# Load order and weight preparation in the scan stage of a two-layer SSD and pooling step

## The chip, the cores and the metric

The program runs on one core of one Trainium2 chip. The metric is the device time of one execution in microseconds (us); a smaller time is better. The time before is the median of three runs. A core has TensorE (PE) for matrix products, VectorE (DVE), ScalarE (ACT) and GpSimd (POOL) for elementwise work, and SyncE (SP), whose instruction queue here does nothing but issue transfers (DMAs). Each engine works through its own queue in order; an instruction that waits holds up all behind it.

## The reference

One inference step of a two-layer trunk on 1024 prompt tokens and 64 new sample tokens (8 sequences of 8), model width 1024. Layer 0 is a Mamba-2 SSD mixer, layer 1 a multi-scale causal pooling mixer. Each is modulated by adaLN and added to a residual. Cut to what matters:

```python
for i in range(DEPTH):                                   # 2 layers
    mod = silu(c) @ ada_w[i] + ada_b[i]                  # adaLN: shift, scale, gate
    hn = rmsnorm(x, norm_g[i]) * (1 + scale) + shift
    out = ssd_branch(hn, ...) if i == 0 else pool_branch(hn, ...)
    x = x + (1 + gate) * out

# ssd_branch
z, xbc, dt = split(hn @ w_in)
conv = conv_b + sum(xp[:, k:k+L] * conv_w[k] for k in range(4)); new_conv = xp[:, -3:]
xs, B, C = split(silu(conv))
y, new_ssm = ssd_scan(xs, softplus(dt + dt_bias), -exp(a_log), B, C, state)   # 8 groups of 4 heads
gated = grouped_rmsnorm((y + d * xs) * silu(z)) * norm_g
out = gated @ w_out
# ssd_scan, per chunk of 128 tokens
y = (C B^T * decay) (x dt) + C exp(acum) h ;  h = exp(acum_end) h + B^T decay_end (x dt)
```

Returned are the outputs for prompt and sample tokens, the SSM states, the last three convolution inputs and the last fifteen pooling inputs of each sequence.

## The kernel before

All data are float32. The big products run as three products of a high part in the type float32r and the rest (`hi*hi`, `hi*lo`, `lo*hi`), so each weight block has to be split by ACT (the high half, a rounded copy) and DVE (the low half, the difference). Activations lie with features on the 128 partitions and the 1088 tokens in the free dimension; many products are made with a Strassen-like scheme on halves of 544 tokens.

The program has these stages: a front (norm, first adaLN blocks, gate and part of the input projection, to about 339 us of the span), the scan stage (339 to about 870 us), the rest of the SSD output projection (to about 1000 us), then the pooling layer.

**The scan stage** (`ssd_layer`, `scan`) loops over the 8 groups `g`, and in each over four phases `p` of 256 tokens. A phase does, in the program's order: `prep_step((g, p))`; fill units (`units(fill, a)`, then `b`, then `c`, the counts come from `PACE`); `scan_front(p+1)`, the transposes of the next phase; `scan_state(p)`, the state update; `scan_decay(p+1)`, the decay matrices of the next phase on ACT and DVE; `scan_y(p)`, the products that give the output; one adaLN block where `ADA` names the phase. At `p == 3` `silu_burst` and the front of the next group follow. A fill unit is one third of a 128-column tile of the input projection of the next group: 24 matmuls (`mm`), some 4 us of PE. Units are what keep PE busy while the scan's chain runs on ACT and DVE. From group 7 on, the units are products of the SSD output projection (`op`).

**Loads.** Nearly every transfer is issued from SP. The pieces named below are:
- `scan_ac` (L542): `acb`, the decay exponents of four heads and 256 tokens, broadcast to all 128 partitions. There is one `acb` buffer, so the next one waits for the last read of the one before, which is `cd` (L583) in `scan_decay`.
- `stream_raw` (L137, L141): the stream of weights through three `wr` buffers. Projection blocks (`wr<-win`) and adaLN blocks (`wr<-adaA`, `wr<-adaG`, two per adaLN block) share it in a fixed order. `stream_next` loads up to three items ahead when a projection tile starts; `ada_block` asks for its own two blocks when it comes to them (`stream_next_raw`).
- `xbd`: projection tiles that the front had made and stored (`MOVED`: tile 1 of groups 1 to 7 and tile 2 of group 7). `proj_group` loads them back (L430) when it passes their place.
- `ncT` (L407): the convolution's edge rows, stored when the last tile of a group is done; they are copied by POOL (L371, L372).
- `hpT` (L606): the final prompt state of a group, stored in `scan_state` at `p == 3`.
- `prep_step`: prepares the first 8 of 28 weight blocks of the output projection, in 16 halves. A half is loaded as two blocks of 256 KB (`wp<-wout`, L1195); DVE adds or subtracts them (L1186) at the next call; at the call after that ACT makes the high half (L1181), DVE the low half (L1182), and 512 KB are stored (`wpd<-wp`, L1183). `PREP` says how many halves start at which call. `ow_load` loads the results back from group 7 on.

**What sets the order.** In the scan stage the PE queue is pinned to the program's order. The other queues are ordered by the framework's scheduler: it plays the program through with a model of the hardware, and each queue takes, of the instructions that the model holds to be ready, the one that is first in the program. So an instruction's place in the program is a priority, and where the hardware is later than the model, the queue waits.

Of the kernel before, what the change touches and what calls it, by code (L numbers as in the profile page):

```python
# [38 lines left out]
PACE = (((0, 1, 1), (0, 1, 1), (0, 1, 1), (0, 1, 2)),) * 6 + (((0, 2, 2), (0, 2, 2), (0, 1, 2), (0, 1, 2)), ((0, 1, 1), (0, 1, 2), (0, 1, 0), (0, 1, 1)))  # L39
ADA = tuple((g, p) for g in range(7) for p in ((0, 1, 2) if g == 0 else (0, 2, 3) if g == 1 else (0, 2, 3) if g == 5 else (0,) if g == 6 else (0, 2)))  # L40
NPREP = 8
PREP = {None: 4, (0, 0): 2, (0, 1): 2, (0, 2): 1, (0, 3): 1, (1, 3): 1, (2, 3): 2, (3, 3): 2, (4, 3): 1}
OWTAGS = (("wr", "wr"), ("wh", "wl"), ("wh", "wl"))
NSLOT_A = 30
NSLOT_B = 7
# [66 lines left out]
class Build:  # L112
# [147 lines left out]
    def ada_block(self, src, raws=None):  # L260

        nc = self.nc
        own = raws = raws or (self.ada_load(src) if src is not None else None)
        raws = [t[:, :1024] for t in raws] if raws else [self.stream_next_raw().rearrange("p a m -> p (a m)") for _ in range(2)]
        pm = self.pp.tile([P, 512], F32, tag=self.amtag, bufs={"mm": 3, "y": 2, "tr": 2}[self.amtag], name=self.name("am"))
        for hh in range(2):
            for j in range(4):
                self.te.matmul(pm[32 * j:32 * j + 32, :256], self.scp[:, j + 4 * hh, :], raws[hh][:, 256 * j:256 * j + 256],
                                 start=(hh == 0), stop=(hh == 1), tile_position=(0, 32 * j))
        if own:  # L270
            self.slots.free(*own)
        mp = self.cp.tile([P, 256], F32, tag="mp", bufs=1, name=self.name("mp"))
        nc.scalar.activation(mp, pm[:, :256], AF.Copy)
        yield
        p2 = pm[:, 256:]
        for i in range(2):
            self.te.matmul(p2[:, 16 * i:16 * i + 9], mp[:, 128 * i:128 * i + 128], self.kc[:, K_SEL9:K_SEL9 + 9], start=True, stop=True)
        yield p2
# [98 lines left out]
    def proj_open(self, g):  # L377
# [2 lines left out]
        ncv = self.gp.tile([P, 4, 9, 3], F32, tag="ncv", bufs=2, name=self.name("ncv"))  # L380
        return dict(g=g, scv=scv, ncv=ncv, ti=(16 + g, 24 + g, 2 * g, 2 * g + 1), out=[])

    def proj_begin(self, G, ii):
        nc = self.nc
        raw = self.raw_tile()
        nc.gpsimd.memset(raw[:, 0:3], 0.0)
        nc.gpsimd.tensor_copy(raw[:, 1027:1115].rearrange("p (b w) -> p b w", w=11)[:, :, 0:3], G["scv"][:, ii])
        return raw

    def proj_end(self, G, ii, raw, ahead=False):  # L390
        dst = self.slots.get("xbc")
        self.conv_tile(G["ti"][ii], raw, dst, G["ncv"][:, ii])
        g, nt = G["g"], self.io["ncT"][G["g"]]
        if ahead:
            self.nc.scalar.activation(dst, dst, AF.Silu)
            self.nc.sync.dma_start(nt[:, ii], G["ncv"][:, ii])
            if (g, ii) in MOVED:
                self.nc.sync.dma_start(self.xbd[g, ii], dst)
                self.slots.free(dst)
                return  # L400
        G["out"].append(dst)
        if ii == 3 and not ahead:
            kept = [i for i in range(4) if (g, i) not in MOVED]
            for a in kept:
                if a - 1 not in kept:
                    n = next(i for i in range(a, 5) if i not in kept)
                    self.nc.sync.dma_start(nt[:, a:n], G["ncv"][:, a:n])  # L407

    def silu_burst(self, s):

# [13 lines left out]
    def proj_group(self, G):  # L424

        nc = self.nc
        for ii in range(4):
            if (G["g"], ii) in MOVED:
                dst = self.slots.get("xbc")
                nc.sync.dma_start(dst, self.xbd[G["g"], ii])  # L430
                G["out"].append(dst)
                continue
            w = self.stream_next()
            raw = self.proj_begin(G, ii)
            if (G["g"], ii) == (7, 3):

                ps = [self.mm_tile() for _ in CH]
                for k in range(8):
                    for c in range(3):
                        self.mm1(ps[c], w, k, self.hn[k], CH[c], k == 0, k == 7)  # L440
                    self.slots.free(*self.hn[k])
                    yield
                for c in range(3):
                    self.proj_evict(G, ii, raw, ps[c], c)
                yield
                return
            for c, (a, n) in enumerate(CH):
                ps = self.mm_tile()
                self.mm3(ps, w, self.hn, CH[c])
                self.proj_evict(G, ii, raw, ps, c)  # L450
                yield
# [136 lines left out]
    def scan_state(self, s, p):  # L588

        nc, gp = self.nc, self.gs  # L590
        _, xd, Bt, cd, _ = s.M[p]
        S = self.pp.tile([P, 512], F32, tag="S", bufs=1, name=self.name("S"))
        for cc in range(2):
            self.te.matmul(S[:, 256 * cc:256 * cc + 256], Bt[:, cc], xd[:, cc, 1].rearrange("p r q -> p (r q)"), start=True, stop=True)
        for cc in range(2):
            h, Sv = s.h[-1], S[:, 256 * cc:256 * cc + 256].rearrange("p (r q) -> p r q", r=4)
            hn = gp.tile([P, 4, 64], F32, tag="h", bufs=3, name=self.name("h"))
            if h is None:
                nc.vector.tensor_copy(hn, Sv)
            else:  # L600
                hd = gp.tile([P, 4, 64], F32, tag="hd", bufs=1, name=self.name("hd"))
                nc.gpsimd.tensor_tensor(out=hd, in0=h, in1=cd[:, :, cc].unsqueeze(2).to_broadcast([P, 4, 64]), op=ALU.mult)  # L602
                nc.vector.tensor_tensor(out=hn, in0=hd, in1=Sv, op=ALU.add)  # L603
            s.h.append(hn)
        if p == 3:
            nc.sync.dma_start(self.io["hpT"][s.g], hn.rearrange("p r q -> p (r q)"))  # L606

    def scan_evac(self, s, q, src, tok):
        y = s.xs[q]
# [566 lines left out]
    def prep_step(self, key):  # L1176
# [10 lines left out]
        new = []  # L1187
        for _ in range(min(PREP.get(key, 0), 2 * NPREP - self.prepn)):
            i, h = divmod(self.prepn, 2)
# [367 lines left out]
    def fills(self):  # L1557

        for g in range(1, 7):
            yield from self.proj_fill(g)  # L1560
        pr = self.proj_fill(7)
        yield from itertools.islice(pr, 9 - 3 * len([i for i in MOVED if i[0] == 7]))
        self.op_begin(0)
        self.optags = ("mm",)
        self.rows = [None] * 16
        blk = self.row_blocks(2, 3)
        for j, _ in enumerate(pr):
            if j == 4:
                self.ow_load()
            for _ in range(99 if j == 7 else 1):  # L1570
                next(blk, None)
            if j < 8:
                yield
        self.ow_load()
        self.x = [None] * 8
        yield from self.out_fill()

# [39 lines left out]
    def scan(self, s, fill):  # L1617

        g = s.g
        last, after = self.scans[g - 1] if g else None, self.scans[g + 1] if g < 7 else None  # L1620
        for p in range(4):
            a, b, c = PACE[g][p]
# [8 lines left out]
            self.scan_state(s, p)  # L1631
            if p < 3:
                self.scan_decay(s, p + 1)
                if p < 2:
                    self.scan_ac(s, p + 2)
                elif after:
                    self.scan_ac(after, 0)
            self.units(fill, b)
            if p == 3 and after:
                self.silu_burst(after)  # L1640
            self.scan_y(s, p, self.sample_y if p == 3 else None)
            if p == 2:
                self.sample_front(s)
                self.sample_inter(s)
# [7 lines left out]
            elif p == 3:  # L1652
                if g < 7:
                    self.sample_decay(s)
                else:
                    self.gate_rows(s)
            self.units(fill, min(c, 1))
            for _ in ada:
                pass
            if p == int(g == 7):  # L1660
# [14 lines left out]
            else:  # L1675
                r = c - min(c, 1)
# [328 lines left out]
```

## Time and profile before

| what | value |
|---|---|
| median of 3 runs | 1622.03 us (1621.26 to 1628.29) |
| the profiled execution | 1621.86 us, of which the span from the first to the last instruction is 1620.0 us |
| PE, DVE, ACT, POOL busy | 1568.6, 1307.7, 803.4, 491.8 us |
| moved by DMA | 295.80 MB, mean 183 GB/s |

How to read it: busy time is the time in which at least one instruction of the engine was under way. PE is the engine with the most. A wait belongs to the engine that waited and names what ended it. The page cuts the span into 40 slices of 40.5 us, so the scan stage is slices 9 to 22.

### The profile page before, as it was taken

How to read it: one execution, taken by the hardware profiler on the slowest of the kernel's cores; microseconds unless marked ns; L12 is line 12 of the kernel's file. 1: busy time of each engine (PE TensorE's matmuls, PEld its weight loads, DVE VectorE, ACT ScalarE, POOL GpSimd, SP SyncE). 2: the span in 40 equal slices, each digit the busy share in tenths (PEclk: the TensorE clock that was granted, in tenths of full speed). 3: DMA queues.
4: the chain of work that ended last, by engine and by line, in shares of the span. 5: the costliest groups of instructions: out<-in, count | busy, mean ns of one | idle time of the engine just before them, and what ended most of it. 6: DMA issues, size and time to landing. Idle time of an engine off the chain costs nothing.

```text
span 1620.0 us, 31607 instructions
## 1 busy us (share of the span) xinstructions
PE 1568.6 (97%) x12495; PEld 1508.3 (93%) x12495; DVE 1307.7 (81%) x2095; ACT 803.4 (50%) x1426; POOL 491.8 (30%) x508
## 2 busy tenths in 40 slices
PE   8999999997999999999998999999999999999997
PEld 6899999996988888988887999999999999999997
DVE  6876787857888889888896999888889867667876
ACT  6663343446667667666653367523232334233355
POOL 0134555511121221111110003765666640000231
PEclk9999999998999999999998999999999999999999
DMA  8422222378675675677889763233323379466673
GB/s 350 164 100 94 87 84 85 111 245 289 225 251 186 207 255 187 215 262 246 320 282 306 194 161 118 71 115 113 115 102 105 108 236 380 135 179 178 162 164 115
DMA packets 118651, 295.80 MB, mean 183 GB/s; under 512 B 22860, under 2 KB 46824, under 8 KB 118504
## 3 DMA queue, kind: packets, MB, share of 16 engines
q1 hardware_dynamic: 110440, 270.32, 48.8%
q0 software_dynamic: 5760, 19.01, 6.7%
q10 hardware_dynamic: 2304, 4.46, 0.7%
q8 instruction: 98, 1.61, 0.4%
q14 instruction: 49, 0.40, 0.1%
HBM read 222.93 MB, written 68.59 MB: 180 GB/s over the span
## 4 chain that ended last, share of the span: by engine, by line
PE 77%; DVE 7%; DMA 7%; ACT 5%; issue 2%; POOL 1%; SPq 0%; DVEq 0%; ACTq 0%; POOLq 0%
PE st L103 32%; PE mm L103 18%; PE op L103 15%; PE y L103 3%; DMA wp<-wout 2%; PE pl L103 2%; DMA acb<-acd 2%; PE S L103 2%; PE am L103 1%; ACT M L580 1%; DMA wr<-pout 1%; PE tr L103 1%; PE ms L103 1%; DVE raw L366 1%; PE tr L106 1%
## 5 line engine op out<-in xcount | busy, mean ns | idle before, releaser
L103 PE MATMUL op<-b,w 128*128 128x272 f32 x2688 | 350.0, 292 | 15.6 <-ACT w L1231 7.1
L103 PEld LDWEIGHTS op<-b,w 128*128 128x128 f32 x2688 | 343.4, 191 | 21.3 <-ACT w L1231 7.7
L103 PE MATMUL st<-hh,w 128*128 128x272 f32 x1664 | 323.2, 289 | 0.0
L103 PEld LDWEIGHTS st<-hh,w 128*128 128x128 f32 x1664 | 265.4, 189 | 0.3 <-issue 0.3
L103 PE MATMUL st<-t,w 128*128 128x272 f32 x1872 | 242.7, 288 | 1.3 <-POOL w L197 1.3
L103 PE MATMUL st<-hl,w 128*128 128x272 f32 x832 | 240.6, 289 | 0.0
L103 PEld LDWEIGHTS st<-t,w 128*128 128x128 f32 x1872 | 237.4, 188 | 1.5 <-POOL w L197 1.5
L103 PE MATMUL mm<-hh,wh 128*128 128x364 f32 (+1 forms) x528 | 183.7, 348 | 2.1 <-ACT wh L160 2.1
L103 PE MATMUL mm<-hh,wl 128*128 128x364 f32 (+1 forms) x528 | 175.1, 332 | 0.3 <-DVE wl L161 0.3
L103 PE MATMUL mm<-hl,wh 128*128 128x364 f32 (+1 forms) x528 | 174.9, 331 | 0.0
L103 PEld LDWEIGHTS st<-hl,w 128*128 128x128 f32 x832 | 156.8, 188 | 0.0
L195 ACT ACTIVATE w<-wr 128x512 fp32r<-128x512 f32 x104 | 65.6, 631 | 179.6 <-PE st L103 143.7
L602 POOL TENSOR_TENSOR hd<-h,cd 128x256 f32<-128x256 f32 x56 | 58.5, 1044 | 225.8 <-DVE h L603 142.5
L103 PEld LDWEIGHTS mm<-hh,wh 128*128 128x128 f32 x528 | 100.7, 191 | 14.0 <-issue 9.5
L366 DVE SCALAR_TENSOR_TENSOR raw<-raw,vec,raw 128x1112 f32<-128x1112 f32 x64 | 91.2, 1426 | 17.5 <-ACT raw L364 17.0
L197 POOL TENSOR_TENSOR w<-wr,w 128x512 fp32r<-128x512 f32 x52 | 91.4, 1757 | 44.2 <-ACT w L195 44.2
L103 PEld LDWEIGHTS mm<-hl,wh 128*128 128x128 f32 x528 | 100.7, 191 | 0.7
L103 PEld LDWEIGHTS mm<-hh,wl 128*128 128x128 f32 x528 | 100.4, 190 | 0.8 <-DVE wl L161 0.8
L1256 DVE SCALAR_TENSOR_TENSOR x<-op,gat,x 128x272 f32<-128x272 f32 (+1 forms) x160 | 73.1, 480 | 26.9 <-PE op L103 23.0
L580 ACT ACTIVATE M<-acb,tka 128x128 f32<-128x128 f32 x256 | 81.1, 389 | 24.6 <-PE y L103 13.1
L974 DVE TENSOR_TENSOR u<-st,u 128x272 f32<-128x272 f32 x174 | 67.6, 411 | 31.6 <-PE st L103 29.8
L197 DVE TENSOR_TENSOR w<-sw,w 128x512 fp32r<-128x512 f32 x78 | 79.2, 1016 | 14.6 <-ACT w L195 14.4
(279 smaller groups left out, 3210.5 us busy)
## 6 DMA issues: line engine op xcount, KB each, us to landing
wr<-win SPq DMA_DIRECT2D x48, 512.0 KB, 4.1
acb<-acd SPq DMA_DIRECT2D x32, 512.0 KB, 4.6
wr<-pin SPq DMA_DIRECT2D x32, 512.0 KB, 3.5
wr<-pout SPq DMA_DIRECT2D x28, 512.0 KB, 4.5
wr<-wout SPq DMA_DIRECT2D x20, 512.0 KB, 5.7
wr<-pout POOLq DMA_DIRECT2D x20, 512.0 KB, 5.9
x<-xT SPq DMA_DIRECT2D x16, 544.0 KB, 6.7
zsd<-z SPq DMA_DIRECT2D x16, 544.0 KB, 2.7
```

The source lines that it names most:

```text
L103: return self.pin(self.build.nc.tensor.matmul(*a, **k))
L106: return self.pin(self.build.nc.tensor.transpose(*a, **k))
L195: self.nc.scalar.activation(hi, src, AF.Copy)
L197: eng.tensor_tensor(out=lo, in0=src, in1=hi.bitcast(F32), op=ALU.subtract)
L366: nc.vector.scalar_tensor_tensor(out=acc[:, :n], in0=raw[:, k:k + n], scalar=w[k], in1=acc[:, :n], op0=ALU.mult, op1=ALU.add)
L580: nc.scalar.activation(M[:, r, t], acb[:, r, t], AF.Relu, bias=self.tka[cc][:, col + r:col + r + 1], scale=-1.0)
L602: nc.gpsimd.tensor_tensor(out=hd, in0=h, in1=cd[:, :, cc].unsqueeze(2).to_broadcast([P, 4, 64]), op=ALU.mult)
L974: nc.vector.tensor_tensor(out=out, in0=x, in1=y, op=ALU.add)
L1256: ins = nc.vector.scalar_tensor_tensor(out=x[e][:, a:a + pn], in0=ps[:, :pn], scalar=g, in1=x[e][:, a:a + pn], op0=ALU.mult, op1=ALU.add)
```

## The change

It changes the places of transfers in the program, and the schedule of the preparation. No arithmetic changes and no transfer is added or taken away.

1. `PREP`: the first call starts 2 halves in place of 4; the calls of scan 0 start 1 each in place of 2, 2, 1, 1; in scans 1 to 5, phases 1 and 3 start 1 each, in place of 1, 2, 2, 1 at phase 3 of scans 1 to 4. The sum stays 16.
2. `ada_block`: right after the products that read two streamed blocks, it issues the loads of up to the next three items of the stream, as far as fewer than three are held.
3. `ncT`: `proj_end` puts the store into a list; it is issued at the next `proj_begin`, or behind group 7's last tile.
4. `xbd`: a stored tile gets its slot and its load when tile 3 of its group starts, not when its own place is passed.
5. `scan_ac`: behind `scan_y`, not behind `scan_decay`, with the fill units `b` between the two.
6. `hpT`: behind the units `c` of phase 3, not in `scan_state`.

```diff
-PREP = {None: 4, (0, 0): 2, (0, 1): 2, (0, 2): 1, (0, 3): 1, (1, 3): 1, (2, 3): 2, (3, 3): 2, (4, 3): 1}
+PREP = {None: 2, **{(g, p): 1 for g in range(6) for p in range(4) if g < 1 or p in (1, 3)}}
...
         if own:
             self.slots.free(*own)
+        else:
+            for i in range(self.wpos, min(self.wpos + 3, len(self.items))):
+                if len(self.wraw) < 3:
+                    self.stream_raw(i)
...
+    late = ()
+
     def proj_begin(self, G, ii):
         nc = self.nc
+        for dst, src in self.late:
+            nc.sync.dma_start(dst, src)
+        self.late = []
...
-                    self.nc.sync.dma_start(nt[:, a:n], G["ncv"][:, a:n])
+                    self.late.append((nt[:, a:n], G["ncv"][:, a:n]))
...
             if (G["g"], ii) in MOVED:
-                dst = self.slots.get("xbc")
-                nc.sync.dma_start(dst, self.xbd[G["g"], ii])
-                G["out"].append(dst)
+                G["out"].append(None)
                 continue
+            if ii == 3:
+                for i in range(3):
+                    if G["out"][i] is None:
+                        G["out"][i] = self.slots.get("xbc")
+                        nc.sync.dma_start(G["out"][i], self.xbd[G["g"], i])
...
             s.h.append(hn)
-        if p == 3:
-            nc.sync.dma_start(self.io["hpT"][s.g], hn.rearrange("p r q -> p (r q)"))
...
         self.ow_load()
+        for dst, src in self.late:
+            self.nc.sync.dma_start(dst, src)
+        self.late = []
...
             if p < 3:
                 self.scan_decay(s, p + 1)
-                if p < 2:
-                    self.scan_ac(s, p + 2)
-                elif after:
-                    self.scan_ac(after, 0)
             self.units(fill, b)
             if p == 3 and after:
                 self.silu_burst(after)
             self.scan_y(s, p, self.sample_y if p == 3 else None)
+            if p < 2:
+                self.scan_ac(s, p + 2)
+            elif p == 2 and after:
+                self.scan_ac(after, 0)
...
             self.units(fill, min(c, 1))
+            if p == 3:
+                self.nc.sync.dma_start(self.io["hpT"][g], s.h[-1].rearrange("p r q -> p (r q)"))
```

## The prediction

> **What bounds the kernel now.** First the page: what is the busiest engine, and where does it fall short? The rows are the span, the engines' busy time, and PE's row of the 40 slices.
>
> ```profile
> span 1620.0 us, 31607 instructions
> ...
> PE 1568.6 (97%) x12495; PEld 1508.3 (93%) x12495; DVE 1307.7 (81%) x2095; ACT 803.4 (50%) x1426; POOL 491.8 (30%) x508
> ...
> PE   8999999997999999999998999999999999999997
> ```
>
> PE bounds it, with 51.4 us short of the span. Its weak slices are the first, the last, the tenth (364 to 405 us) and the 22nd, at the end of the scan stage. So the scan stage, 339 to 880 us, is cut by the windows view (columns: window, length, busy time of PE, PEld, DVE, ACT, POOL, granted clock, DMA share, GB/s).
>
> ```profile
> 339.00:384.00 45.00, 44.82 (x348) 42.40 (x346) 30.29 (x50) 24.41 (x53) 4.26 (x7) 1.00 0.94 322
> 384.00:400.00 16.00, 5.99 (x25) 4.63 (x26) 10.86 (x13) 10.13 (x22) 2.00 (x5) 0.68 0.79 257
> 400.00:544.00 144.00, 142.84 (x1251) 130.91 (x1251) 116.41 (x172) 94.97 (x195) 26.68 (x50) 1.00 0.70 229
> 544.00:560.00 16.00, 12.68 (x95) 11.95 (x92) 14.35 (x20) 10.33 (x20) 1.53 (x1) 0.89 0.52 181
> 560.00:745.00 185.00, 182.38 (x1577) 167.07 (x1576) 157.61 (x225) 127.30 (x265) 34.88 (x67) 1.00 0.66 221
> 745.00:764.00 19.00, 17.89 (x148) 15.46 (x148) 16.92 (x28) 11.50 (x30) 4.88 (x4) 0.91 0.90 308
> 764.00:784.00 20.00, 16.42 (x156) 14.33 (x153) 13.90 (x19) 12.63 (x30) 4.40 (x7) 0.91 0.77 236
> 784.00:856.00 72.00, 69.30 (x647) 63.72 (x646) 70.17 (x128) 41.13 (x85) 10.49 (x10) 1.00 0.86 307
> 856.00:880.00 24.00, 16.33 (x114) 15.21 (x114) 13.31 (x26) 6.33 (x12) 2.27 (x3) 0.79 1.01 316
> ```
>
> The windows sum to 541 us with 508.6 us of PE: 32.4 us idle, a third of it (10.0 us) in the 16 us from 384. Everything else the change could save on PE is in these 32 us and in the slow clock behind the long gaps. The view of waits, for this stage, says what ended PE's gaps.
>
> ```profile
> PE am L103 <- DMA wr<-adaG: 7.7, 1, 7.7
> PE op L103 <- ACT w L1231: 6.3, 1, 6.3
> PE tr L106 <- ACT xbc L412: 4.7, 3, 2.4
> PE op L103 <- ACT raw L456: 3.6, 1, 3.6
> ```
>
> The largest is one late transfer: an adaLN block. The timeline of SP (start, duration, instruction) shows why it was late, and the chain shows PE's pace behind the gap.
>
> ```profile
> 375.86 0.39 SPq L542 DMA_DIRECT2D acb<-acd  x1
> 376.35 1.98 SPq L1183 DMA_DIRECT2D wpd<-wp  x2
> 378.43 3.54 SPq L1195 DMA_DIRECT2D wp<-wout  x4
> 385.75 0.38 SPq L542 DMA_DIRECT2D acb<-acd  x1
> 386.18 0.50 SPq L141 DMA_DIRECT2D wr<-adaG  x1
> 386.77 0.38 SPq L137 DMA_DIRECT2D wr<-win  x1
> ```
> ```profile
> 396.07 5.39 PE mm L103 x22
> 403.82 3.97 PE mm L103 x24
> ```
>
> SP was free at 381.97 and stood for 3.8 us in front of a broadcast whose single buffer ACT had not finished reading; the adaLN block and the next projection block, both needed at once, stood behind it.
>
> **The change, part by part.** All against the profiled execution, 1621.86 us (1620.0 of span and 1.86 around it); it lies 0.2 us under the median of 1622.03, so no correction is made.
>
> **1. First stall (edits to `PREP`, `ada_block`, `scan_ac`).** Behind the 7.7 for the adaLN block PE waited for the split of the projection block that was issued behind it:
>
> ```profile
> PE mm L103 <- ACT wh L160: 2.1, 1, 2.1
> ```
>
> Then comes the slow clock. 22 matmuls at the later pace (3.97/24 = 0.165 each) are 3.6 us and took 5.39: 1.8 lost, and some 0.7 more is my estimate for the 10 us before, at clock 0.68. 7.7 + 2.1 + 2.5 = 12.3 us. Three edits work on it:
> - `ada_block` issues the second half of block (0, 1) and the next projection block right after the products of block (0, 0), about a phase before they are used, and no longer behind the fourth broadcast.
> - Scan 0 no longer carries 10 halves (4+2+2+1+1) but 6. By 400 us, 9 halves had been loaded; it will be 5. Four halves are 4 x (2 x 256 + 512 KB) = 4.2 MB loaded and stored. At 0.94 busy for 322 GB/s a fully busy set of DMA engines moves 343 GB/s, so 12.2 us of its time go out of the stretch 339 to 400, which had 45 x 0.94 + 16 x 0.79 = 54.9. The first broadcast, which stood behind four of these loads, lands some us earlier too, and the chain broadcast, ACT, broadcast moves with it.
> - The broadcast moves behind `scan_y`: it competes less with what PE needs next.
>
> Bounds: 0 (another load becomes the late one) to 12.3. After a removal of 12.2 us of DMA work and some 10 us of time the stretch is still (54.9 - 12.2)/(61 - 10) = 0.84 busy, so I do not take all of it: **-10**.
>
> **2. Stalls at the end of each scan (`PREP`).** Here is the end of scan 2, with two halves begun at (2, 3).
>
> ```profile
> 540.31 0.69 DVE L1186 TENSOR_TENSOR wp<-wp 128x512 f32<-128x512 f32 x1 [2.35 <-DMA wp<-wout]
> ...
> 544.62 0.69 DVE L1186 TENSOR_TENSOR wp<-wp 128x512 f32<-128x512 f32 x1 [1.89 <-DMA wp<-wout]
> ...
> 545.69 0.44 PE L103 MATMUL y<-ea,h 128*64 128x128 f32 x4 [0.95 <-DVE h L603]
> ...
> 553.23 1.33 PE L106 MATMUL tr<-kc,xbc 128*128 128x128 f32 x5 [2.37 <-ACT xbc L412]
> ```
>
> DVE stands in front of a sum whose blocks have not landed; ACT, which has the high part to make of that sum, stands behind it; the eviction, the convolution and SiLU of the next group's last tile come late, and PE waits for them: 0.95 and 2.37. The second half costs DVE 1.89 + 0.69 for the sum and about 0.7 for the low part, 3.3 in all, which is what PE lost. The wait row `tr <- xbc` has three: 2.37 here, so 4.7 - 2.37 = 2.3 for the other two, scan 3 (two halves) and scan 4 (one). I put 1.4 on the first and **0.9** on the second, and take 0.9 for every scan's end with one half. The slow clock: 0.89 over 16 us is 11% of the pulses, 1.4 us on the 12.7 us of PE. Scan 2: 3.3 + 1.4 becomes 0.9, -3.8. Scan 3: 1.4 becomes 0.9, -0.5. Scans 1 and 4 keep one half. Scan 5 gets one, +0.9. Sum **-3.4**; bounds -7 (4.7 + 1.4 + 0.9, the ends of scans 2 to 5 clean) to +0.9 (scans 2 and 3 as now, scan 5 new).
>
> **3. Halves at phase 1 of scans 1 to 5**, new places. The halves of phases 0 to 2 of scan 0 were worked off with PE idle for 1.2 us in all of 400 to 544: in mid-scan 3 to 4 us of held ACT are covered by the three `mm` buffers and a unit of 4 us. **0**, bounds 0 to 5 x 0.95. If that cover went, each would cost what scan 2 shows for its first gap.
>
> **4. Later places of stores and loads.** The two longest waits of SP's queue in this stage, and one row of the DMA issues (count, KB each, us to landing):
>
> ```profile
> SPq L542 <- ACT cd L583: 84.6, 20, 8.6
> SPq L407 <- POOL raw L387: 51.2, 12, 6.6
> ```
> ```profile
> xbc<-xbd SPq DMA_DIRECT2D x8, 544.0 KB, 8.9
> ```
>
> 136 us of SP's standing are addressed here, but SP's time is not PE's: in 400 to 544 and 560 to 745 PE lost 3.8 us together, with all these waits in place. `ncT` and `hpT` feed nothing here: **0**, bounds -1 to +1. A stored tile comes back three units later, which is over 12 us; it is used at the end of the scan, over 20 us on, and takes 8.9: **0**. The later broadcast: a queue place behind a 512 KB projection block is 1.5 us at 343 GB/s, and ACT has no use for it for a phase: **0**, bounds 0 to +12 (the slower rival).
>
> **5. Stalls from 745 us on** (6.3 for `w`, 3.6 for `raw`): no edit touches what they wait for. **0**, bounds -15 to +5 (the rivals).
>
> Sum: -10 - 3.4 = -13.4; 1621.9 - 13.4 = 1608.5, taken as **1609**.
>
> [...]
>
> **The rivals.**
>
> **A. The stall only moves.** For it: DMA at 0.94 before the gap; what is prefetched sooner makes something else later, and the broadcasts at 375.86 and 385.75 show a chain (landing, ACT, next broadcast) with a pace of 10 us per phase. Against it: 12 us of DMA work leave. Then term 1 gives 0 to -4 and term 2 holds: 1614 to 1622, say **1618**.
>
> **B. The late broadcast holds ACT.** ACT's queue is in order, and evictions of PE's tiles stand in it behind reads of `acb`. It happens now:
>
> ```profile
> 769.64 0.40 ACT L580 ACTIVATE M<-acb,tka 128x128 f32<-128x128 f32 x1 [3.50 <-DMA acb<-acd]
> ```
>
> ACT stood 3.5 us, and PE waited 3.6 for `raw` L456 right behind, plus 0.09 x 16.4 = 1.5 of slow clock: 5.1 us each. Three such more eat the 13.4; five give 1608.5 + 25.5 = **1634**. Against it: ACT stands for the broadcast in most phases already, and PE lost by it once. [...]
>
> **C. The end of the stage gains too.** SP's standing for `hpT` has one long case:
>
> ```profile
> SPq L606 <- DVE h L603: 22.2, 8, 9.9
> ```
>
> It lies in scan 7. If output weights are issued earlier for its absence, the 6.3 of `w` and its slow clock (0.21 x 16.3 = 3.4) go: 1609 - 10 = **1599**. Against it: those loads wait for `wr` buffers that PE frees, and DMA is at 1.01 there.
>
> **How the numbers follow.** Forecast 0.50, A 0.24, B 0.10, C 0.16. The forecast's own range is 1603 to 1614. The range leaves out most of B and the far half of C: **1597 to 1622**. A measurement of this kernel tells 0.5% (8 us, below 1614 or above 1630) from no change: faster **0.64**, same **0.27**, slower **0.09**.
>
> **What would show it.** Right: no PE gap over 2 us between 370 and 400 and the clock at 1.00 there; SP's adaLN loads ahead of the broadcasts; at the ends of scans 1 to 5 gaps near 0.9 each; from 745 on the same stalls, some 13 us earlier. Wrong: a wait of `am`, `mm` or `y` of several us in scan 0 (A); ACT standing for `acb` like the 3.5 us above in several scans, with PE waiting for `raw` (B); new gaps in phase 1 of scans 1 to 5 (term 3).

## The result and the profile after

The changed kernel took 1606.94 us (median of four runs, 1603.06 to 1609.0); the kernel before took 1621.64 us on the same chip. The ratio is 0.9898, with a 95% interval of 0.9865 to 0.993. In a second set of runs the same program gave 1609.82 us and 0.9919 (0.9896 to 0.9942). So the change is worth some 13 to 15 us, and the forecast of 1609 us lies between the two medians.

The profiled execution took 1607.27 us. First its page: span, busy times and PE's row of the 40 slices.

```profile
span 1605.5 us, 31619 instructions
...
PE 1566.8 (98%) x12495; PEld 1506.3 (94%) x12495; DVE 1306.5 (81%) x2095; ACT 802.8 (50%) x1426; POOL 487.6 (30%) x508
...
PE   8999999999999999999998999999999999999997
```

The span is 14.5 us shorter. PE's idle time went from 51.4 to 38.7 us (-12.7), its busy time fell by 1.8. The tenth slice went from 7 to 9, and the 22nd still shows the weak place at the end of the stage. The windows view of the changed kernel says where the time went (columns as before: window, length, busy time of PE, PEld, DVE, ACT, POOL, granted clock, DMA share, GB/s; the windows are cut by time, and from about 400 us on the work lies up to 16 us earlier than before).

```profile
339.00:384.00 45.00, 45.00 (x346) 43.52 (x346) 29.48 (x49) 26.45 (x58) 4.85 (x8) 1.00 0.93 311
384.00:400.00 16.00, 16.00 (x168) 14.33 (x168) 14.31 (x21) 11.28 (x27) 4.46 (x8) 1.00 0.89 302
...
339.00:865.00 526.00, 507.35 (x4355) 465.86 (x4354) 442.39 (x679) 338.44 (x706) 90.89 (x153) 0.98 0.77 259
```

In the 16 us from 384, PE is busy for all 16.00 us in place of 5.99, at clock 1.00 in place of 0.68. The DMA share there did not fall: 0.93 and 0.89, against 0.94 and 0.79. The scan stage as a whole is 526 us in place of 541: 18.7 us of PE idle in place of 32.4 (-13.7), and 507.35 us of PE busy in place of 508.6 (-1.3). Since the span fell by 14.5, the rest of the program gave back 0.5 us. The waits view names what still ends PE's gaps in this stage (total, times, longest). `am` are the adaLN products and `mp` is ACT's copy of them, `tr` the transposes, `op` the output projection with its weights `w`, `raw` a projection tile as ACT evicts it, `xbc` the finished tile.

```profile
PE op L103 <- ACT w L1241: 6.3, 1, 6.3
PE op L103 <- ACT raw L468: 3.8, 1, 3.8
PE am L103 <- ACT mp L277: 2.8, 3, 1.4
```

The 7.7 for the adaLN block, the 2.1 for its neighbour's split and the 4.7 of `tr <- xbc` are gone; the late waits for `w` and `raw` stand as they were. SP's timeline around the old stall:

```profile
372.74 0.39 SPq L554 DMA_DIRECT2D acb<-acd  x1
373.17 0.51 SPq L141 DMA_DIRECT2D wr<-adaG  x1
373.77 0.38 SPq L137 DMA_DIRECT2D wr<-win  x1
```

The second half of the adaLN block was asked for at 373.17 us, where it had been 386.18: 13 us sooner. It still goes out right behind a broadcast, but behind the third one and not the fourth.

### The profile page after: what moved, and what is told of

Its sections match the earlier page's. It is cut to its first block, busy times and chain, and to the rows that moved or that the text cites. A ratio compares the mean times of both kernels' runs of the same rounds, so it can differ in the third digit from the quotient of the medians.

```text
span 1605.5 us, 31619 instructions
## 1 busy us (share of the span) xinstructions
PE 1566.8 (98%) x12495; PEld 1506.3 (94%) x12495; DVE 1306.5 (81%) x2095; ACT 802.8 (50%) x1426; POOL 487.6 (30%) x508
## 4 chain that ended last, share of the span: by engine, by line
PE 77%; DMA 7%; DVE 6%; ACT 5%; issue 3%; POOL 1%; SPq 0%; DVEq 0%; ACTq 0%; POOLq 0%
PE st L103 33%; PE mm L103 18%; PE op L103 15%; PE y L103 2%; PE pl L103 2%; DMA wp<-wout 2%; DMA acb<-acd 2%; ACT M L592 1%; PE S L103 1%; PE am L103 1%; DMA wr<-pout 1%; PE tr L103 1%; PE tr L106 1%; PE p L103 1%; PE ms L103 1%
## 5 line engine op out<-in xcount | busy, mean ns | idle before, releaser
L614 POOL TENSOR_TENSOR hd<-h,cd 128x256 f32<-128x256 f32 x56 | 51.3, 917 | 225.2 <-DVE h L615 150.7
```

## The experiments

Twelve runs were made, in three sets. Each set has its own runs of the kernel before; ratios are to those, with a 95% interval.

| run | what it is | median (range), us | before, us | ratio |
|---|---|---|---|---|
| prep_only | before, with the new `PREP` alone | 1616.79 (1614.73 to 1617.05) | 1623.4 | 0.9955 (0.994 to 0.997) |
| order_only | changed kernel, old `PREP` | 1611.05 (1608.41 to 1619.23) | 1623.4 | 0.9931 (0.9909 to 0.9952) |
| all_but_acb | changed kernel, old place of the broadcast | 1611.8 (1607.47 to 1613.61) | 1623.4 | 0.9923 (0.9906 to 0.994) |
| all_but_ada | changed kernel, no loads in `ada_block` | 1613.51 (1612.67 to 1616.01) | 1623.4 | 0.994 (0.9925 to 0.9955) |
| changed_again | changed kernel | 1609.82 (1607.51 to 1614.43) | 1624.06 | 0.9919 (0.9896 to 0.9942) |
| prep_p02 | changed kernel, halves at phases 0 and 2 | 1609.4 (1608.24 to 1612.38) | 1624.06 | 0.991 (0.9891 to 0.993) |
| evict62 | changed kernel, one decay behind an eviction | 1605.85 (1604.37 to 1608.24) | 1624.06 | 0.9892 (0.9874 to 0.9911) |
| both | prep_p02 and evict62 together | 1610.86 (1604.76 to 1612.92) | 1624.06 | 0.9915 (0.989 to 0.9941) |
| ada_only | before, with the loads in `ada_block` alone | 1612.62 (1610.71 to 1613.13) | 1624.93 | 0.9923 (0.9899 to 0.9948) |
| acb_only | before, with the later broadcast alone | 1625.24 (1619.08 to 1628.49) | 1624.93 | 0.9999 (0.9982 to 1.0017) |
| all_but_stores | changed kernel, old places of `ncT` and `hpT` | 1603.5 (1602.23 to 1606.26) | 1624.93 | 0.9873 (0.9851 to 0.9896) |
| all_but_xbd | changed kernel, old place of the stored tiles' loads | 1612.51 (1608.64 to 1613.09) | 1624.93 | 0.9922 (0.9899 to 0.9944) |

### Which edit removes the first stall

The prediction credited three edits. Each was tried alone, and each was undone alone.

**The preparation alone** (prep_only):

```diff
-PREP = {None: 4, (0, 0): 2, (0, 1): 2, (0, 2): 1, (0, 3): 1, (1, 3): 1, (2, 3): 2, (3, 3): 2, (4, 3): 1}
+PREP = {None: 2, **{(g, p): 1 for g in range(6) for p in range(4) if g < 1 or p in (1, 3)}}
```

> The kernel before with the new PREP alone. Theory (the first stall is bytes and order together, the scan ends are the halves begun at phase 3): 4.2 MB leave scan 0, the broadcast chain moves some 4 us earlier, but the adaLN block still stands behind the fourth broadcast, so 2 to 4 of the 7.7 us stay; scan 2's end loses its two gaps of 0.95 and 2.37. Sum 8 to 12 us faster, 1610 to 1614. Rival (order alone did it): the stall at 384 stays within 2 us of its 7.7 and the time is 1617 to 1622. Rival (bytes alone did it): stall gone, 1605 to 1609, no different from all edits together.

It gave 0.9955, less than expected. Its waits of PE in the stage, and two rows of SP's timeline:

```profile
PE tr L106 <- ACT xbc L412: 3.2, 3, 1.7
PE y L103 <- DVE h L599: 2.6, 1, 2.6
PE mm L103 <- DVE wl L161: 2.1, 1, 2.1
```
```profile
373.55 0.39 SPq L542 DMA_DIRECT2D acb<-acd  x1
...
375.05 0.38 SPq L141 DMA_DIRECT2D wr<-adaG  x1
```

The 7.7 us wait is gone: the block now goes out behind the third broadcast. The DMA share from 339 to 384 us is 0.94, as before, so what the trace shows is a new order in SP's queue; that the missing transfers led the schedule to it is argued, not shown. A wait of 2.1 for a split is left. The end of scan 2 loses its two gaps but for 0.25, as expected. But the ends of scans 3 and 4 wait 1.27 and 1.70 for `xbc`, the end of scan 5 waits 1.23 for `mp`, and a new wait of 2.6 for the state `h` has come in scan 6. The stall is 7.7 us shorter, and the span only 5.0 (1615.0 us).

**The order alone** (order_only, the changed kernel with the old `PREP`):

```diff
-PREP = {None: 2, **{(g, p): 1 for g in range(6) for p in range(4) if g < 1 or p in (1, 3)}}
+PREP = {None: 4, (0, 0): 2, (0, 1): 2, (0, 2): 1, (0, 3): 1, (1, 3): 1, (2, 3): 2, (3, 3): 2, (4, 3): 1}
```

> All edits but PREP, which has its old values. Theory (bytes and order together): the adaLN block is issued a phase earlier, so the wait of am for it goes, but scan 0 keeps its 10 halves and DMA stays at 0.94: 2 to 4 us of PE waits for other late loads stay in scan 0, and the ends of scans 1 to 4 lose their old 5.6 us (0.95 + 0.95 + 2.37 + 1.4 less one). Sum 8 to 10 us faster, 1611 to 1614. Rival (bytes did it): the stall moves to another load, 1617 to 1622. Rival (order did it all): scan 0 clean, and only the ends stay, 1608 to 1610.

0.9931. The block is asked for at 370.31, ahead of the broadcast at 375.10, and PE has no gap worth naming in scan 0 up to 469 us, although scan 0 carries all ten halves. The 2 to 4 us of waits for other late loads that were expected there did not come; in this the rival was right. The ends of scans keep their waits:

```profile
PE tr L106 <- ACT xbc L421: 4.4, 3, 1.8
PE am L103 <- ACT mp L277: 4.2, 3, 2.7
```

**The four lines in `ada_block` alone** (ada_only):

```diff
         if own:
             self.slots.free(*own)
+        else:
+            for i in range(self.wpos, min(self.wpos + 3, len(self.items))):
+                if len(self.wraw) < 3:
+                    self.stream_raw(i)
```

> The kernel before with the loads ahead in ada_block alone. Theory now (of bytes and order either is enough for the first stall, and of the order edits it is this one): the second half of block (0, 1) is issued a phase earlier and the 7.7 us wait of am goes, with the 2.1 behind it; the scan ends keep their gaps; 9 to 13 us faster than before. Rival (it takes the broadcast's later place too): the block still stands behind a broadcast, 2 to 5 us of the stall stay, 4 to 8 us faster.

0.9923, which can't be told from all six edits together (0.9919). Its windows, SP's timeline and waits:

```profile
339.00:384.00 45.00, 44.98 (x347) 43.14 (x345) 31.20 (x51) 24.53 (x51) 4.54 (x7) 1.00 0.95 322
384.00:400.00 16.00, 16.00 (x166) 14.15 (x162) 13.69 (x22) 12.09 (x28) 2.80 (x7) 1.00 0.90 321
```
```profile
371.09 0.33 SPq L141 DMA_DIRECT2D wr<-adaG  x1
...
376.68 0.38 SPq L546 DMA_DIRECT2D acb<-acd  x1
...
386.60 0.38 SPq L546 DMA_DIRECT2D acb<-acd  x1
```
```profile
PE tr L106 <- ACT xbc L416: 5.5, 3, 2.6
...
PE am L103 <- ACT mp L277: 5.2, 3, 2.7
```

This is the clearest row pair of the study. Ten halves are in scan 0, the DMA engines are busy for 0.95 and 0.90 of the two windows, the broadcasts go out within 1 us of where they went before (375.86 and 385.75), and PE is idle for 0.02 us in all. The stretch was full, but bytes were not what made the block late; its place in SP's queue was. The ends of scans are no better than before.

**All but these four lines** (all_but_ada, the diff above taken back out of the changed kernel):

> All edits but the loads ahead in ada_block. Theory (bytes and order together): the second half of block (0, 1) is asked for only when it is used, behind the broadcast; am in scan 0 waits 2 to 5 us, 1609 to 1613. Rival (bytes alone, or the broadcast's place alone): no wait of am for a DMA over 1 us, 1604 to 1609, as with all edits.

0.994. The expected wait of `am` did not come: the block went out at 375.00, behind the third broadcast. PE has small gaps in scan 0, the largest a wait of 1.4 us for a split:

```profile
PE tr L106 <- ACT xbc L417: 3.6, 4, 1.3
...
PE y L103 <- DVE h L607: 2.6, 1, 2.6
...
PE mm L103 <- DVE wl L161: 1.4, 1, 1.4
```

It looks like prep_only: the same three waits. Together the four runs say that `PREP` and the loads in `ada_block` are two ways to remove the same stall: of PE's gaps of 7.7 and 2.1 us the loads alone take all, `PREP` alone all but 2.1. In time the two are not equal (0.9923 and 0.9955). SP's queue sorts all fourteen profiles of this study: the stall of over 7 us stands in the two where the block goes out behind the fourth broadcast (the kernel before and acb_only, below), and in none of the twelve where it goes out behind the second or the third.

**The later broadcast alone** (acb_only), and **all but it** (all_but_acb). The first moves `scan_ac` in the kernel before, the second moves it back in the changed kernel:

```diff
                 self.scan_decay(s, p + 1)
-                if p < 2:
-                    self.scan_ac(s, p + 2)
-                elif after:
-                    self.scan_ac(after, 0)
...
             self.scan_y(s, p, self.sample_y if p == 3 else None)
+            if p < 2:
+                self.scan_ac(s, p + 2)
+            elif p == 2 and after:
+                self.scan_ac(after, 0)
```

> The kernel before with the broadcast's later place alone. Theory now: the adaLN block is asked for behind the broadcast in both places, so its wait stays within 2 us of 7.7 and the time within 3 us of before. Rival (the later broadcast frees the queue): the stall falls below 4 us, 5 to 10 us faster. Rival B (the later broadcast holds ACT's evictions): waits for raw or Bt of 2 us and more in several scans, 5 us or more slower.

> All edits but the broadcast's later place: scan_ac stands behind scan_decay again. Theory: the broadcast's place is worth nothing, since it waits for cd in both places and ACT has a phase of slack: within 2 us of all edits, 1604 to 1610. Rival (the broadcast in front of the adaLN and projection loads made the first stall): the stall at 384 comes back in part, 3 to 8 us, 1610 to 1615. Rival (the late broadcast costs ACT): 2 to 5 us faster than all edits, 1602 to 1605.

acb_only gave 0.9999. all_but_acb gave 0.9923, a little slower than it was expected to be but no different from the changed kernel in its second set (0.9919), and PE has no gap over 0.9 us in scan 0. The first stall of acb_only:

```profile
PE am L103 <- DMA wr<-adaG: 7.3, 1, 7.3
...
PE mm L103 <- ACT wh L160: 2.1, 1, 2.1
```

It is the stall of before to within 0.5 us: the broadcast still went out at 386.35 and the block at 386.78. A later place in the program is a lower priority only among instructions that the schedule holds to be ready at once; here it changed nothing. The third edit that the prediction credited had no part in it.

### Stores and stored tiles

**Old places of the stores** (all_but_stores):

```diff
-                    self.late.append((nt[:, a:n], G["ncv"][:, a:n]))
+                    self.nc.sync.dma_start(nt[:, a:n], G["ncv"][:, a:n])
...
             s.h.append(hn)
+        if p == 3:
+            nc.sync.dma_start(self.io["hpT"][s.g], hn.rearrange("p r q -> p (r q)"))
...
-            if p == 3:
-                self.nc.sync.dma_start(self.io["hpT"][g], s.h[-1].rearrange("p r q -> p (r q)"))
```

> The changed kernel with the stores of ncT and hpT back at their old places. Theory (SP's standing for them is not PE's time): within 3 us of the changed kernel on the other chips' ratio, 0.988 to 0.994 of before. Rival (the 74 us of SP's standing for POOL and DVE delay loads that PE needs): loads of projection or adaLN blocks late again, PE waits of 2 us and more for them, 0.995 of before and up.

0.9873, the lowest time of all and just under the expected range. Its interval overlaps that of the changed kernel's first set and only touches that of its second, so the later stores may even have cost time. Its page:

```profile
span 1600.4 us, 31616 instructions
...
PE 1562.0 (98%) x12495; PEld 1500.3 (94%) x12495; DVE 1303.3 (81%) x2095; ACT 801.7 (50%) x1426; POOL 490.2 (31%) x508
```

PE is idle for 38.4 us (38.7 in the changed kernel), so the stores' places did not change what PE waits for. The 5 us are in PE's busy time: the mean granted clock was 0.996, against 0.990. In windows of 2 us over the scan stage the clock's missing pulses add up to 1.7 us here and to 10.2 us in the changed kernel. Why this program kept the higher clock was not settled; the last section shows how loosely the clock follows the gaps.

**Old place of the stored tiles' loads** (all_but_xbd):

```diff
-                G["out"].append(None)
+                dst = self.slots.get("xbc")
+                nc.sync.dma_start(dst, self.xbd[G["g"], ii])
+                G["out"].append(dst)
                 continue
-            if ii == 3:
-                for i in range(3):
-                    if G["out"][i] is None:
-                        G["out"][i] = self.slots.get("xbc")
-                        nc.sync.dma_start(G["out"][i], self.xbd[G["g"], i])
```

> The changed kernel with the stored tiles loaded back at their old place. Theory (a tile comes back a scan ahead of its use in both places): within 3 us of the changed kernel, 0.988 to 0.994 of before. Rival (544 KB in front of the adaLN or projection loads in scan 0 make these late): PE waits of 1 us and more for am or mm between 370 and 400, 0.994 of before and up.

0.9922, not to be told from the changed kernel. `am` waited 2.1 us for `mp` at 391 us, which looks like the rival's sign, but the next run shows 1.9 us there with the edit in place.

### What is left: the ends of scans and the wait for `raw`

**The same program again** (changed_again), as the measure of what repeats:

> The changed kernel as it is, on the same chip as the three kernels below, as their measure. It should give 1604 to 1610, 13 to 17 us under the kernel before on this chip, with no PE gap over 1 us between 340 and 470, and the stalls of 3.8 (raw) and 6.3 (w) in scans 6 and 7.

```profile
PE am L103 <- ACT mp L277: 7.8, 6, 2.4
...
PE op L103 <- ACT raw L468: 2.4, 1, 2.4
```

The same instructions in the same order waited 7.8 us for `mp` in six gaps, where the first profile had 2.8 in three, and 2.4 for `raw`, where it had 3.8. One of the six gaps, 1.9 us at 391 us, lies in the stretch where no gap over 1 us was expected, and the wait for `w` was 5.0 in place of 6.3. This profiled execution was the slowest of its set, 1614.43 us. So a few us in such small waits need not be the effect of an edit.

**Halves at phases 0 and 2** (prep_p02). If a half begun at phase 3 costs 0.9 at the scan's end, moving it removes that:

```diff
-... if g < 1 or p in (1, 3)}}
+... if g < 1 or p in (0, 2)}}
```

> The changed kernel with the halves of scans 1 to 5 begun at phases 0 and 2 in place of 1 and 3. Theory (a half begun at phase 3 holds DVE and ACT in front of the next group's last convolution): the waits of am for mp at the ends of scans 1 and 5, 1.1 and 1.4 us, go, and no new gap over 0.5 us comes in scans 1 to 5; 2 to 4 us faster than the changed kernel. Rival (the two waits come from SiLU and the table loads at a scan's end, whatever the halves do): they stay within 0.5 us and the time is the same within 1.5 us. Rival (any phase has this price): gaps of about 1 us at other phases.

0.991, no gain. Its waits for `mp`:

```profile
PE am L103 <- ACT mp L277: 6.2, 6, 1.6
```

The wait at the end of scan 5 is gone, and no half is under way there: the last one is summed at 704 us. The one at the end of scan 1 stays (1.09 us), but a half does stand there. It begins at (2, 0) in the program, its sum came at 476.71 us, ahead of PE's gap at 481.70, and ACT waited for it:

```profile
477.44 0.64 ACT L1191 ACTIVATE wp<-wp 128x512 fp32r<-128x512 f32 x1 [3.85 <-DVE wp L1196]
```

So the new places in the program did not take the halves away from the ends of scans 1 to 4, and this run does not settle what a half at a scan's end costs. New waits of about 1 us stand elsewhere (0.94 and 1.07 at 531 and 591 us).

**The last decay behind the eviction** (evict62). In the changed kernel ACT's and PE's timelines show the mechanism of the slower rival once, at 753 us:

```profile
753.25 0.40 ACT L592 ACTIVATE M<-acb,tka 128x128 f32<-128x128 f32 x1 [2.62 <-DMA acb<-acd]
...
757.42 0.45 ACT L468 ACTIVATE raw<-mm 128x364 f32<-128x364 f32 x1
...
757.92 2.41 PE L103 MATMUL op<-b,w 128*128 128x272 f32 x9 [3.79 <-ACT raw L468]
```

ACT stands 2.62 us for a broadcast, then works off the decay, and the eviction that PE waits for (`raw` L468) comes behind it. The edit puts that one decay behind the units and behind the last eviction:

```diff
-            nc.scalar.activation(raw[:, 1027:1115] ...
+            self.last_evict = nc.scalar.activation(raw[:, 1027:1115] ...
...
+            late = (g, p) == (6, 2)
-            if p < 3:
+            if p < 3 and not late:
                 self.scan_decay(s, p + 1)
             self.units(fill, b)
+            if late:
+                with self.tc.issue_after(self.last_evict.ins):
+                    self.scan_decay(s, p + 1)
```

> The changed kernel with the decay of scan 6's last phase issued on ACT behind the three evictions of the last projection tile. Theory (rival B's mechanism: ACT, in order, holds evictions behind reads of a broadcast that has not landed): the 3.8 us wait of op for raw and its slow clock go, 3 to 5 us faster than the changed kernel. Rival (the eviction waits for its own products, or the decay then becomes the late one): a wait of 2 us or more of y or S for M or Bt takes its place and the time is the same within 1.5 us.

PE's wait at that place, in PE's timeline of this kernel:

```profile
758.20 3.26 PE L103 MATMUL op<-b,w 128*128 128x272 f32 x24 [0.67 <-ACT raw L468]
```

3.79 became 0.67, and the run with both edits has no such wait, while the twelve profiles with the old order have 1.2 to 4.0. So the order of ACT's queue was the cause. A new wait of 1.0 us of `tr` for `xd` at 786 us came with the edit and took a part of the gain back. The median is 4 us below that of changed_again, but the intervals overlap, so the gain in time is likely and not shown.

**Both together** (both, the last two diffs):

> Both edits together on the changed kernel: halves at phases 0 and 2, and scan 6's last decay behind the evictions. Theory: the two gains are at different places and add, 5 to 9 us faster than the changed kernel, 1598 to 1602. Rival (the time saved ahead of the transfers of scan 7 comes back there, where DMA is at 1.0): less than 3 us faster, with the wait of op for w longer than its 6.3 us.

0.9915: the wait for `raw` is gone here too, yet PE waited 2.3 us for `xbc` at one scan's end and 5.8 for `mp`. The gains did not add.

## Why the prediction was right, step by step

**Term 1, the first stall (-10 taken, bounds 0 to -12.3): right, mis-sized by about 1 to 2 us.** All of it went. PE's gaps of 7.7 and 2.1 are 0, and PE's busy time in the stage fell by 1.3 net: 11.1 by these numbers, 12.3 with the estimate of 2.5. Other slow stretches came and went, each with 1.7 us of pulses missing: those from 553, 754 and 775 us in the kernel before, and from 720, 757 and 805 us in the changed one. (In the second profile of the same program a wait of 1.9 for `mp` stands near the place.) The step that held back some 2 us was "the stretch is still 0.84 busy, so I do not take all of it". The share is in fact 0.93 and 0.89, and PE did not wait. ada_only shows it sharper, at 0.95 and 0.90. At these shares the DMA engines had work, and yet the transfer that was needed next was not late.

Credit was given to three edits. Two of them carry it, each without the other: the loads in `ada_block` (0.9923 alone) and `PREP` (0.9955 alone, and its remaining stall is 2.1 us). The broadcast's place had no part (0.9999 alone). One of the marks named ahead, the adaLN load ahead of the broadcasts, came out for order_only and ada_only but not for the changed kernel, where it went out behind the third broadcast and was early enough there.

**Term 2, the ends of the scans (-3.4): right in sign, close in size in part by luck, wrong in its price.** Before, the gaps at the ends of scans 1 to 4 were 0.95, 0.95 + 2.37, 1.43 and 0.87: 6.6 us. After, scans 2 to 4 are clean, and scans 1 and 5 show, in PE's timeline:

```profile
478.56 0.61 PE L103 MATMUL am<-kc,mp 128*128 128x9 f32 x4 [1.13 <-ACT mp L277]
```
```profile
718.77 0.61 PE L103 MATMUL am<-kc,mp 128*128 128x9 f32 x4 [1.44 <-ACT mp L277]
```

That is 2.6, so -4.0, while the slow clock behind the gap of scan 2 went (1.7 us of pulses missing from 553 us on) and one of the same size came behind the gap of scan 5 (1.7 us from 720 us on). The forecast had -2.0 of gaps and -1.4 of slow clock, so two errors met in its sum. "0.9 us for every scan's end with one half" is not what happened: scans 2 to 4 have one half and no gap, scans 1 and 5 have 1.13 and 1.44.

What the prediction read off scan 2 (a sum that comes late holds ACT, and PE's work comes late behind it) holds, but by these profiles the price goes by what stands behind the half and by how late its blocks land. Scans 1 and 5 are the two with an adaLN block at phase 3 (`ADA`). In scan 1, ACT waits for the half's sum, and the copy `mp` that PE needs comes behind it:

```profile
472.42 0.63 ACT L1191 ACTIVATE wp<-wp 128x512 fp32r<-128x512 f32 x1 [5.85 <-DVE wp L1196]
...
478.13 0.38 ACT L277 ACTIVATE mp<-am 128x256 f32<-128x256 f32 x1
```

In the eight profiles where a half begins at (5, 3), PE waits 1.2 to 2.2 us for `mp` at the end of scan 5; in the six where none does, it does not wait there. (At the end of scan 1 it is less strict: in evict62 ACT waited 4.29 us for the half and PE had no gap.) At the ends of scans 2 to 4, DVE waited 2.4 to 2.9 us for the first half's blocks before, and 0 to 1.1 in the two profiles of the changed kernel. Where `PREP` or the `ada_block` loads are missing (prep_only, order_only, ada_only, all_but_ada) it waited 2.0 to 3.6 us, and waits of up to 1.7, 1.9, 2.6 and 1.3 us for `xbc` stay. So the clean ends need both edits, and none of the other four by itself. Whether the two alone are enough, and why the blocks land sooner with both, was not tested.

**Term 3, halves at phase 1 (0): held.** No gap of 0.3 us or more stands in mid-scan in scans 1 to 5 of the first profile.

**Term 4, later stores, loads and broadcasts (0): held.** acb_only (0.9982 to 1.0017) bounds the broadcast at some 3 us either way, and all_but_xbd and all_but_stores show no loss without their edits. SP's standing in the same stage, by the waits view of the changed kernel:

```profile
SPq L554 <- ACT cd L595: 99.0, 22, 9.7
...
SPq L392 <- POOL raw L396: 28.0, 8, 6.5
...
SPq L1672 <- DVE h L615: 18.4, 8, 9.6
```

The stores' standing fell from 51.2 to 28.0 and from 22.2 to 18.4, that of the broadcasts rose from 84.6 to 99.0. As predicted, SP's time was not PE's, in either direction.

**Term 5, stalls from 745 us on (0): held.** 6.3 stayed 6.3, 3.6 became 3.8, both some 16 us earlier. That they agree so closely is chance: the second profile of the same program has 5.0 and 2.4.

**The sum.** PE's idle time: -9.8 in scan 0 and -4.0 at the ends make -13.8; the windows say -13.7. The small gaps that came and went later cancel: a wait of 1.28 for `h` at 741 us is new, waits of 1.11 and 0.80 are gone. With -1.3 of busy time and +0.5 outside the stage it is -14.5 of span. The forecast was -13.4.

**The rivals.** A fell: nothing of several us took the stall's place. Where the `ada_block` loads are missing, 1.4 to 2.1 us of it do move to a split, so A was true in a small part for prep_only and all_but_ada. B's mechanism is real, as evict62 shows (3.79 became 0.67), but it stood once in the kernel before (3.6 us) and stands once in the changed one (3.8); the later broadcast did not multiply it. C fell: the store of `hpT` was moved and the 6.3 for `w` stayed (5.0 in the second profile).

## What to carry to other kernels

When a transfer is late, read the queue that issues it before its bytes: four lines that ask for a block one step sooner were worth as much as the whole reordering, as far as the intervals can tell, on DMA engines that stayed 0.90 to 0.95 busy. A new place in the program is not yet a new time: the broadcast moved alone went out where it had (at 386.35 us, against 385.75), and a half moved to the next scan's first phase was still worked off at the end of the scan before, so look in the trace where the work went. Two edits that remove the same stall are substitutes, so try each alone before all are kept; four of the six showed no effect that could be measured. Run the same program twice before a gap of 1 us is explained, since small waits came and went between executions of one program (`mp`: 2.8 us in three gaps, then 7.8 in six).

## What was not expected of the hardware

In these profiles the slow clock came in pieces of one size, 1.71 us of missing pulses, and a piece could follow a gap of 1.11 us. In windows of 1 us, the kernel before has five slow stretches from 339 to 880 us: three miss 1.71 us of pulses, and two, from 389 and 863 us, miss three times as much, 5.12. In windows of 2 us, seven profiles (the kernel before, both of the changed kernel, ada_only, prep_p02, evict62 and all_but_stores) each miss a whole multiple of 1.71 us in this stage to within 0.02 us, from 1 (all_but_stores) to 9 (the kernel before). Windows of the kernel before, behind a gap of 1.11 us at 751 us:

```profile
752.00:754.00 2.00, 1.88 (x18) 1.50 (x20) 1.51 (x4) 1.66 (x4) 0.81 (x1) 1.00 0.90 352
754.00:756.00 2.00, 2.00 (x13) 1.62 (x8) 2.00 (x4) 0.00 (x0) 0.81 (x1) 0.58 0.89 209
756.00:758.00 2.00, 2.00 (x11) 1.93 (x10) 2.00 (x4) 0.66 (x1) 0.00 (x0) 0.57 0.99 302
758.00:760.00 2.00, 2.00 (x16) 1.90 (x13) 1.85 (x4) 1.47 (x3) 0.00 (x0) 1.00 1.03 417
```

0.42 x 2 + 0.43 x 2 = 1.7 us of pulses are missing; the lowest clock seen in any window is 0.50, and by an estimate from these two numbers (1.7 / 0.50) the stretch is 3.4 us long. The changed kernel, around three gaps of 0.58, 0.81 and 0.37 us between 800 and 804 us:

```profile
798.00:802.00 4.00, 3.29 (x22) 2.77 (x20) 4.00 (x7) 2.52 (x4) 0.00 (x0) 1.00 0.97 316
802.00:806.00 4.00, 2.82 (x23) 2.07 (x23) 4.00 (x12) 0.76 (x2) 0.09 (x1) 0.89 0.77 285
806.00:810.00 4.00, 4.00 (x34) 3.67 (x31) 4.00 (x8) 2.34 (x8) 0.52 (x1) 0.68 1.00 408
```

0.11 x 4 + 0.32 x 4 = 1.7 again. The kernel before has the same three gaps (0.58, 0.80, 0.37 at 817 to 821 us), and so has all_but_stores; in both the clock stayed at 1.00. Windows of all_but_stores:

```profile
800.00:804.00 4.00, 2.66 (x20) 1.88 (x22) 4.00 (x10) 1.38 (x2) 0.00 (x0) 1.00 0.95 332
804.00:808.00 4.00, 4.00 (x45) 3.73 (x42) 4.00 (x10) 2.80 (x9) 0.62 (x1) 1.00 1.02 417
```

So gaps of 1.11 us, or of 1.76 us in three parts, were followed by a loss of 1.7 us here, and the same three gaps by none in the kernel before (1.75 us in all) and in all_but_stores (1.76). What made the difference was not shown.
